# State updates of sample sequences on 32-row groups of the TensorE array, in place of zero-padded 128-row tiles

## The chip, the cores and the metric

The kernel runs on one core of a Trainium2 chip. The metric is the device time of one execution in microseconds (us); lower is better. Times of a kernel are given as the median of several runs.

## What is computed

One decoder layer: gated linear attention (GLA) beside causal pooling, merged by gates, then a feed-forward block. It runs for one prompt of 256 tokens and for eight sample sequences of 8 new tokens each, which share all weights. The change lies in the GLA state of the samples. Cut to what matters (`D_MODEL` is 2048, so there are 4 heads with `DK_HEAD` 256 and `DV_HEAD` 512, and `DEC_BATCH` is 8):

```python
kd = k * jnp.exp(b_last - b)              # decayed keys
decay = jnp.exp(b_last[:, :, :, 0, :])
...
def step(s, inp):
    qe_n, kd_n, v_n, dec_n = inp
    o = jnp.einsum('bhcd,bhde->bhce', qe_n, s)
    s = dec_n[..., None] * s + jnp.einsum('bhcd,bhce->bhde', kd_n, v_n)
    return s, o
```

For each sample sequence and each head the new state is a 256x512 matrix: the old one times a decay per row, plus the product of the sequence's decayed keys (tokens x 256) with its values (tokens x 512).

## The kernel before, in words

**The bulk.** Activations lie transposed, features on partitions, with all 320 tokens (256 of the prompt, 64 of the samples) along the free axis. Every projection is a stream of matmuls on 128x128 weight tiles and 320 columns. To reach float32 accuracy each weight chunk is split into a high and a low part in the `float32r` format (`split`, L142: ACT writes `whi` at L147, DVE writes `wlo` at L148), and three matmuls stand in place of one (`mm3`, L160: L161 `whi`·high, L162 `whi`·low, L163 `wlo`·high). This stream fills TensorE (PE) nearly from end to end. It is called the main stream below.

**The side work.** After the first head's projections, the loop over heads 1 to 3 (L904) runs the main stream of one head while the attention and pooling steps of the head before it are mixed in: `queue` holds small functions, and `pump` (L887) calls ten of them after each projection. `gla_steps` (L541) makes the list. The Tile scheduler then decides the order on each engine from its own time model, so that the side work's matmuls stand one by one or in small groups between those of the main stream. Their results go to PSUM tiles `pm` of 128x512, one bank each, of which there are four in turn (`misc`, L98).

**The state update.** The eight sequences are handled in two halves `gg` of four sequences `j`. Each sequence owns 32 rows: `kdP` holds its decayed keys (8 high parts, the same again, the 8 low parts, the same again), and `vp` (L665) its values in the matching arrangement, so that one product over 32 rows gives the product at full accuracy. `s_kpn(gg)` (L683) turns the keys of four sequences round by two transposes (`tr`, L123, whose matmul is recorded at L125) and then builds `kpn`, of shape 128 x 4 x 256: POOL clears it (L686), and for each `j` the 32 rows of that sequence are copied into column block `j`, by DVE (L694) for odd `j` and by ACT (L696) for even `j`. All other rows of block `j` stay zero. `s_state(gg, d, j0)` (L762) then takes, for two sequences, the matmul of L767: weights are 128 rows by 128 columns of `kpn`, the moving operand all 128 rows of `vp` by 512 columns; the zeros take out the three other sequences. DVE adds the result to the decayed state (L769), and when the second pair of a tile is done POOL issues the store (L771). Per head there are 2 halves x 2 column blocks `d` x 4 sequences, 64 such matmuls in the program. The page names `kpn` as `w`, after its pool tag.

**Tiles of the array.** Four other places hand a `tile_position` to a matmul: L221 and L281 (conditioning), L645 (attention of the prompt) and L746 (read-out of the sample states). All of these use weights of 32 columns at column offset 0, 32, 64 or 96 and all 128 rows, four side by side. No place uses a row offset.

Of the kernel before, what the change touches and what calls it, by code (L numbers as in the profile page):

```python
# [11 lines left out]
F32 = mybir.dt.float32  # L12
F32R = mybir.dt.float32r
# [7 lines left out]
P = 128  # L21
# [7 lines left out]
H, DK, DV = 4, 256, 512  # L29
# [50 lines left out]
def body(tc, A):  # L80
# [13 lines left out]
    def nm(s):  # L94
        uid[0] += 1
        return "%s_%d" % (s, uid[0])

    def misc():  # L98
        return pmisc.tile([P, 512], F32, tag="m", name=nm("pm"))

    V, S, G, PE = nc.vector, nc.scalar, nc.gpsimd, nc.tensor
# [21 lines left out]
    def tr(out, in_):  # L123
        k = in_.shape[0]
        PE.transpose(out, in_, ident[:k, :k])  # L125
# [273 lines left out]
    with tc.tile_pool(name="head", bufs=1) as xp:  # L399
# [9 lines left out]
        pt = misc()  # L409
# [22 lines left out]
        pt = misc()  # L432
# [105 lines left out]
    def w4(shape, dt=F32):  # L538
        return lp.tile(shape, dt, tag="w4", bufs=4, name=nm("w4"))

    def gla_steps(g):  # L541
        h = g.h
        st = []
        E = {}
# [137 lines left out]

        def s_kpn(gg):  # L683
            def f():
                kpn = E["kpn"] = w4([P, 4, DK], F32R)
                G.memset(kpn.bitcast(F32), 0.0)  # L686
                pt = misc()
                for d in range(2):
                    tr(pt[:, d * P:(d + 1) * P],
                       kdP[:, d, 4 * gg:4 * gg + 4, :].rearrange("p b r -> p (b r)").bitcast(F32))  # L690
                for j in range(4):
                    sl = slice(32 * j, 32 * j + 32)
                    if j % 2:
                        V.tensor_copy(kpn[sl, j, :], pt[sl, 0:DK])  # L694
                    else:
                        S.copy(kpn[sl, j, :], pt[sl, 0:DK])  # L696
            return f

        def s_o(e2):
# [62 lines left out]
        def s_state(gg, d, j0):  # L762
            def f():
                t = E["S0", gg, d]
                for j in (j0, j0 + 1):
                    pt = misc()
                    PE.matmul(pt, lhsT=E["kpn"][:, j, d * P:(d + 1) * P], rhs=E["vp"][:, gg], start=True, stop=True)  # L767
                    c = 4 * gg + j
                    V.scalar_tensor_tensor(t[:, j], t[:, j], E["dec"][:, d, c:c + 1], pt, op0=ALU.mult, op1=ALU.add)  # L769
                if j0 == 2:  # L770
                    nc.gpsimd.dma_start(A["o_gs"][0, 4 * gg:4 * gg + 4, h, d * P:(d + 1) * P, :]  # L771
                                        .rearrange("b p e -> p b e"), t)
            return f
# [119 lines left out]
    st, E = gla_steps(g0)  # L893
# [10 lines left out]
    for h in range(1, H):  # L904
        pump(RATE)
        g = new_group(h)
        for ui, (kind, i, col) in enumerate(units(h)):
# [5 lines left out]
            if kind == "u":  # L913
                pump(len(queue))
                st, E = gla_steps(g)
# [96 lines left out]
    for pi, (f0, f1) in enumerate(parts):  # L1012
# [31 lines left out]
        for ui in range(8):  # L1044
            ps = proj(wdn, 256 * ui, f0, f1, ah, al)
            for i in range(2):
                k = 2 * ui + i
                residual(ps, i, k, 5)
                if pi == 1:
# [3 lines left out]
                    pt = misc()  # L1053
# [9 lines left out]
    pt = misc()  # L1063
# [9 lines left out]
    for a in range(3):  # L1073
        n = P if a < 2 else TS
        for c in range(2):
            sl = yn[a][:n, c * 1024:(c + 1) * 1024]
# [28 lines left out]
```

## Time and profile before

| what | value |
|---|---|
| device time, median of 3 runs | 1989.61 us (1988.78 to 1991.63) |
| span of the profiled execution | 1989.4 us |
| PE busy | 1938.0 us, 97% of the span |
| DVE busy | 1002.8 us, 50% |
| ACT busy | 829.4 us, 42% |
| POOL busy | 179.3 us, 9% |
| matmuls | 13808 |

The profile is of one execution, whose own time is its span, from the first instruction to the last. PE is the matmul, PEld the loading of its weights, which can go on beside the matmul before it. A matmul's row shows its duration from start to modelled end, which includes the time through the array, so that neighbours overlap: a main stream matmul is listed at 0.31 us though one ends every 0.15 us. The chain of waits is the view that shows how far one instruction moves the end: each of its pieces runs from the end of the piece before it to its own end.

### The profile page before, as it was taken

The page shows a single profiled execution, that of the slowest core. Times are in us where ns is not written, and L with a number is a line of the kernel's source. Part 1 is how long each engine was busy: PE and PEld are TensorE (multiplying, and loading weights), DVE is VectorE, ACT ScalarE, POOL GpSimd, SP SyncE. Part 2 cuts the span into 40 slices and gives each one's busy share as a digit, 9 for nine tenths or more (in the row PEclk, how much of TensorE's full clock was granted, in tenths as well). Part 3 has the DMA queues.
Part 4 walks back from the last instruction along what each step waited for, and adds up shares of the span by engine and source line. Part 5 has one row for each costly group of instructions (what it writes and reads, how often), then busy time and mean ns, then how long its engine had stood idle before and what let it go on. Part 6 is the DMA issues. An engine that isn't in the chain of part 4 may idle for free.

```text
span 1989.4 us, 34665 instructions
## 1 busy us (share of the span) xinstructions
PE 1938.0 (97%) x13808; PEld 1819.7 (91%) x13808; DVE 1002.8 (50%) x1918; ACT 829.4 (42%) x1483; POOL 179.3 (9%) x292
## 2 busy tenths in 40 slices
PE   5999999999999999999999999999999999999997
PEld 3778998889999889989979999999999999999997
DVE  2655645656356635665574444444444444444554
ACT  3323633544336433653344333433333434344443
POOL 1002101212121112111130000000000000000000
PEclk9999999999999999999999999999999999999998
DMA  9997458758975888479836555444444444444443
GB/s 316 344 333 239 141 170 281 231 182 288 302 221 171 274 283 257 148 248 329 265 100 197 185 185 178 156 147 145 150 148 154 149 151 151 152 150 140 149 141 101
DMA packets 309276, 400.59 MB, mean 201 GB/s; under 512 B 12418, under 2 KB 273058, under 8 KB 308778
## 3 DMA queue, kind: packets, MB, share of 16 engines
q1 hardware_dynamic: 279754, 291.17, 46.8%
q0 software_dynamic: 29360, 107.21, 15.6%
q8 instruction: 108, 1.77, 0.4%
q14 instruction: 54, 0.43, 0.1%
HBM read 373.90 MB, written 24.67 MB: 200 GB/s over the span
## 4 chain that ended last, share of the span: by engine, by line
PE 90%; DMA 6%; DVE 2%; ACT 1%; issue 0%; SPq 0%; POOL 0%; ACTq 0%; DVEq 0%
PE ps L161 26%; PE ps L163 26%; PE ps L162 26%; PE pm L281 3%; DMA araw<-w_ada 2%; DMA raw<-w_in 2%; PE pm L125 2%; PE pm L221 1%; DMA raw<-w_o 1%; PE pm L767 1%; PE pm L746 1%; PE pm L715 1%; DMA vr<-b_ada 1%; DVE wlo L148 1%; ACT whi L147 0%
## 5 line engine op out<-in xcount | busy, mean ns | idle before, releaser
L148 DVE TENSOR_TENSOR wlo<-raw,whi 128x512 fp32r<-128x512 f32 x952 | 654.9, 692 | 804.8 <-ACT whi L147 801.3
L147 ACT CAST whi<-raw 128x512 fp32r<-128x512 f32 x952 | 586.2, 622 | 923.3 <-PE ps L162 811.2
L161 PE MATMUL ps<-hh,whi 128*128 128x320 f32 x1408 | 443.1, 315 | 4.2 <-ACT whi L147 3.2
L162 PE MATMUL ps<-hl,whi 128*128 128x320 f32 x1408 | 439.2, 312 | 0.0
L163 PE MATMUL ps<-hh,wlo 128*128 128x320 f32 x1408 | 436.6, 312 | 1.3 <-DVE wlo L148 1.3
L161 PE MATMUL ps<-h2h,whi 128*128 128x320 f32 x1408 | 435.7, 310 | 0.0
L162 PE MATMUL ps<-h2l,whi 128*128 128x320 f32 x1408 | 435.5, 309 | 0.0
L163 PE MATMUL ps<-h2h,wlo 128*128 128x320 f32 x1408 | 435.4, 309 | 0.0
L161 PEld LDWEIGHTS ps<-hh,whi 128*128 128x128 f32 x1408 | 264.9, 188 | 28.2 <-issue 16.2
L163 PEld LDWEIGHTS ps<-hh,wlo 128*128 128x128 f32 x1408 | 264.2, 188 | 13.7 <-issue 7.3
L162 PEld LDWEIGHTS ps<-hl,whi 128*128 128x128 f32 x1408 | 265.1, 188 | 5.4 <-issue 4.6
L161 PEld LDWEIGHTS ps<-h2h,whi 128*128 128x128 f32 x1408 | 264.3, 188 | 3.4 <-ACT ah L317 3.4
L162 PEld LDWEIGHTS ps<-h2l,whi 128*128 128x128 f32 x1408 | 264.3, 188 | 0.0
L163 PEld LDWEIGHTS ps<-h2h,wlo 128*128 128x128 f32 x1408 | 264.3, 188 | 0.0
L161 PE MATMUL ps<-ah,whi 128*128 128x320 f32 x704 | 217.7, 309 | 0.0
L162 PE MATMUL ps<-al,whi 128*128 128x320 f32 x704 | 216.5, 308 | 0.0
L163 PE MATMUL ps<-ah,wlo 128*128 128x320 f32 x704 | 216.5, 308 | 0.0
L162 PEld LDWEIGHTS ps<-al,whi 128*128 128x128 f32 x704 | 132.0, 187 | 0.0
L161 PEld LDWEIGHTS ps<-ah,whi 128*128 128x128 f32 x704 | 131.9, 187 | 0.0
L163 PEld LDWEIGHTS ps<-ah,wlo 128*128 128x128 f32 x704 | 131.9, 187 | 0.0
L255 POOL DMA_DIRECT2D araw<-w_ada x64 | 54.9, 862 | 448.5 <-PE pm L281 419.2
L161 PE MATMUL ps<-mh,whi 128*128 128x320 f32 x256 | 79.5, 310 | 0.7 <-ACT whi L147 0.7
(280 smaller groups left out, 1609.4 us busy)
## 6 DMA issues: line engine op xcount, KB each, us to landing
raw<-w_gu SPq DMA_DIRECT2D x176, 512.0 KB, 3.5
raw<-w_in SPq DMA_DIRECT2D x173, 512.0 KB, 4.5
araw<-w_ada POOLq DMA_DIRECT2D x64, 1024.0 KB, 8.5
raw<-w_down SPq DMA_DIRECT2D x80, 512.0 KB, 3.5
raw<-w_ada SPq DMA_DIRECT2D x64, 512.0 KB, 6.6
S<-state_gla POOLq DMA_DIRECT2D x16, 1024.0 KB, 9.6
o_gs<-S POOLq DMA_DIRECT2D x16, 1024.0 KB, 5.9
raw<-w_o SPq DMA_DIRECT2D x32, 512.0 KB, 5.1
```

The source lines that it names most:

```text
L125: PE.transpose(out, in_, ident[:k, :k])
L147: S.copy(hi, raw)
L148: V.tensor_sub(lo, raw, hi.bitcast(F32))
L161: PE.matmul(ps, lhsT=whi, rhs=xhi, start=start, stop=False)
L162: PE.matmul(ps, lhsT=whi, rhs=xlo, start=False, stop=False)
L163: last_mm[:] = [PE.matmul(ps, lhsT=wlo, rhs=xhi, start=False, stop=stop).ins]
L221: PE.matmul(ps[32 * j:32 * j + 32, 0:w], lhsT=scT[:, k0 + i, :], rhs=raw[:, i, :], start=r == 0, stop=r == 3, tile_position=(0, 32 * j))
L255: nc.gpsimd.dma_start(t[:, r:r + step], wada[:, k0 + r:k0 + r + step, col:col + nb * P])
L281: PE.matmul(ps[32 * j:32 * j + 32, 0:w], lhsT=scT[:, k0 + r + j, :], rhs=ada_raw[n][:, r + j, :], start=k0 == 0 and first, stop=k0 + nk == ...
L715: PE.matmul(pt, lhsT=E["kdn"][:, s, d * P:(d + 1) * P], rhs=E["vn"][:, s], start=s == 0, stop=s == 1)
L746: PE.matmul(pt[32 * j:32 * j + 32, :], lhsT=qeP[:, d, 4 * gg + j, :], rhs=E["S0", gg, d][:, j], start=False, stop=d == 0, tile_position=(0 ...
L767: PE.matmul(pt, lhsT=E["kpn"][:, j, d * P:(d + 1) * P], rhs=E["vp"][:, gg], start=True, stop=True)
```

## The change

`kpn` becomes one unpadded tile of 128 x 256: the transposed keys of four sequences are copied into it as they are, by one ACT copy, and neither the clearing nor the three other copies are made. Each matmul of `s_state` takes as weights only the 32 rows of its sequence, and as moving operand the same 32 rows of `vp`, and is placed at row offset 32·j of the array by `tile_position`. The two matmuls of a pair are written before the two DVE updates instead of in turn with them; their two `pm` tiles are taken together.

```diff
         def s_kpn(gg):
             def f():
-                kpn = E["kpn"] = w4([P, 4, DK], F32R)
-                G.memset(kpn.bitcast(F32), 0.0)
+                kpn = E["kpn"] = w4([P, DK], F32R)
                 pt = misc()
                 for d in range(2):
                     tr(pt[:, d * P:(d + 1) * P],
                        kdP[:, d, 4 * gg:4 * gg + 4, :].rearrange("p b r -> p (b r)").bitcast(F32))
-                for j in range(4):
-                    sl = slice(32 * j, 32 * j + 32)
-                    if j % 2:
-                        V.tensor_copy(kpn[sl, j, :], pt[sl, 0:DK])
-                    else:
-                        S.copy(kpn[sl, j, :], pt[sl, 0:DK])
+                S.copy(kpn, pt[:, 0:DK])
             return f
...
         def s_state(gg, d, j0):
             def f():
                 t = E["S0", gg, d]
-                for j in (j0, j0 + 1):
-                    pt = misc()
-                    PE.matmul(pt, lhsT=E["kpn"][:, j, d * P:(d + 1) * P], rhs=E["vp"][:, gg], start=True, stop=True)
+                pts = [misc(), misc()]
+                for j, pt in zip((j0, j0 + 1), pts):
+                    r = slice(32 * j, 32 * j + 32)
+                    PE.matmul(pt, lhsT=E["kpn"][r, d * P:(d + 1) * P], rhs=E["vp"][r, gg], start=True, stop=True,
+                              tile_position=(32 * j, 0))
+                for j, pt in zip((j0, j0 + 1), pts):
                     c = 4 * gg + j
                     V.scalar_tensor_tensor(t[:, j], t[:, j], E["dec"][:, d, c:c + 1], pt, op0=ALU.mult, op1=ALU.add)
```

The changed lines shift those below: the matmul of L767 is L762 after. How the scheduler places the matmuls is seen in the order on PE. At the start of a group of eight (the first head, `gg` 0; `pm` is the result, `vp` the values, `w` is `kpn`, `ps` the main stream's result) PE has before:

```order
L125 MATMUL pm_3220<-cst,adasb_3221 128x128 x2
L767 MATMUL pm_3229<-vp_2953,w_506_2981 128x512
L767 MATMUL pm_3232<-vp_2953,w_506_2981 128x512
L767 MATMUL pm_3235<-vp_2953,w_506_2981 128x512
L162 MATMUL ps_3321<-hl_104,whi_3340 128x320
```

and after:

```order
L125 MATMUL pm_3216<-cst,adasb_3217 128x128 x2
L762 MATMUL pm_3225<-vp_2953,w_506_2981 128x512
L762 MATMUL pm_3226<-vp_2953,w_506_2981 128x512
L762 MATMUL pm_3231<-vp_2953,w_506_2981 128x512
L162 MATMUL ps_3317<-hl_104,whi_3336 128x320
```

Nothing has moved here: the first pair and the first of the second pair stand side by side in both. All eight groups of eight begin so. The five others of the same group stand, some 20 rows on, before:

```order
L161 MATMUL ps_3321<-hh_91,whi_3374 128x320
L767 MATMUL pm_3238<-vp_2953,w_506_2981 128x512
L162 MATMUL ps_3321<-hl_107,whi_3374 128x320
L163 MATMUL ps_3321<-hh_91,wlo_3375 128x320
L161 MATMUL ps_3321<-hh_92,whi_3374 128x320
L162 MATMUL ps_3321<-hl_108,whi_3374 128x320
L767 MATMUL pm_3242<-vp_2953,w_506_2981 128x512
L163 MATMUL ps_3321<-hh_92,wlo_3375 128x320
L161 MATMUL ps_3321<-hh_92,whi_3374 128x320
L162 MATMUL ps_3321<-hl_108,whi_3374 128x320
L767 MATMUL pm_3245<-vp_2953,w_506_2981 128x512
L163 MATMUL ps_3321<-hh_92,wlo_3375 128x320
```

and after:

```order
L161 MATMUL ps_3317<-hh_91,whi_3370 128x320
L762 MATMUL pm_3232<-vp_2953,w_506_2981 128x512
L162 MATMUL ps_3317<-hl_107,whi_3370 128x320
L163 MATMUL ps_3317<-hh_91,wlo_3371 128x320
L161 MATMUL ps_3317<-hh_92,whi_3370 128x320
L162 MATMUL ps_3317<-hl_108,whi_3370 128x320
L762 MATMUL pm_3238<-vp_2953,w_506_2981 128x512
L163 MATMUL ps_3317<-hh_92,wlo_3371 128x320
L161 MATMUL ps_3317<-hh_92,whi_3370 128x320
L162 MATMUL ps_3317<-hl_108,whi_3370 128x320
L762 MATMUL pm_3239<-vp_2953,w_506_2981 128x512
L163 MATMUL ps_3317<-hh_92,wlo_3371 128x320
```

Here too the order stays: each of these five stands alone between main stream matmuls, the two of a pair (`pm_3238` and `pm_3239` after) with three matmuls of the main stream between them. Over the whole program the 64 matmuls stand in 48 places, 8 of three and 40 of one, in both kernels.

Elsewhere on PE one thing moves twice (heads 1 and 2): a run of eight column-tiled matmuls of L645. Before, it is whole:

```order
L162 MATMUL ps_4684<-hl_104,whi_4703 128x320
L645 MATMUL pm_4100<-w_706_4104,EQK_3942 32x128 x3
L645 MATMUL pm_4100<-EQK_3942 32x128
L645 MATMUL pm_4100<-w_706_4104,EQK_3942 32x128 x3
L645 MATMUL pm_4100<-EQK_3942 32x128
L163 MATMUL ps_4684<-hh_88,wlo_4704 128x320
```

After, one matmul of the main stream stands in its middle:

```order
L162 MATMUL ps_4668<-hl_102,whi_4671 128x320
L645 MATMUL pm_4088<-w_706_4092,EQK_3934 32x128 x3
L645 MATMUL pm_4088<-EQK_3934 32x128
L163 MATMUL ps_4668<-hh_86,wlo_4672 128x320
L645 MATMUL pm_4088<-w_706_4092,EQK_3934 32x128 x3
L645 MATMUL pm_4088<-EQK_3934 32x128
L161 MATMUL ps_4668<-hh_86,whi_4671 128x320
```

So the runs of column-tiled matmuls number 92 before and 94 after.

## The prediction

> **What bounds the kernel now.** I read the page first, then the table of stages, then the chain of waits in the stage of the change. The page's first lines, and the chain's shares by line:
>
> ```profile
> span 1989.4 us, 34665 instructions
> PE 1938.0 (97%) x13808; PEld 1819.7 (91%) x13808; DVE 1002.8 (50%) x1918; ACT 829.4 (42%) x1483; POOL 179.3 (9%) x292
> PE 90%; DMA 6%; DVE 2%; ACT 1%; issue 0%; SPq 0%; POOL 0%; ACTq 0%; DVEq 0%
> ```
>
> PE is busy for 97% of the span and holds 90% of the chain. An average may hide stages, so the table by stages comes next, cut at 270 and 900 us, since the 64 matmuls of L767 start between 302.5 and 871.3 us:
>
> ```profile
> core 0: us, PE busy (x) PEld busy (x) DVE busy (x) ACT busy (x) POOL busy (x), PEclk, DMA share, GB/s
> 270.00:900.00 630.00, 624.08 (x4637) 564.29 (x4637) 345.55 (x685) 283.50 (x524) 109.10 (x157) 1.00 0.74 239
> ...
> L767 PEld LDWEIGHTS pm<-vp,w x64: 187/188/192, 302.5 to 871.2; 128*128 128x128 f32 x64
> L767 PE MATMUL pm<-vp,w x64: 388/393/482, 302.5 to 871.3; 128*128 128x512 f32 x64
> ```
>
> In this stage PE stands idle for 630.0 − 624.1 = 5.9 us, while DVE is busy for 55%, ACT for 45% and POOL for 17% of it. So PE alone sets the end here: what PE gains or loses between 270 and 900 us, the kernel gains or loses, and what the other engines gain is worth nothing as long as PE does not come to wait for them. What an instruction of PE costs is its piece in the chain:
>
> ```profile
> 302.53 0.22 PE pm L125 x2
> 302.75 0.71 PE pm L767 x3
> 303.46 0.15 PE ps L162
> ...
> 305.96 0.15 PE ps L161
> 306.11 0.23 PE pm L767
> 306.34 0.15 PE ps L162
> ```
>
> A state matmul costs 0.23 us, alone or in a row of three (0.71 us, of which the first holds 0.01 more); one of the main stream costs 0.15 us. There is no loss at the border between the two: both are whole-array matmuls, and the next weights (0.19 us to load, the row above) are loaded beside the running matmul. All 64 together take about 64 x 0.23 = 14.7 us of PE's time.
>
> **The change part by part.** *The copies and the clearing.* These rows of the groups by shape are the work around `kpn`:
>
> ```profile
> L686 POOL MEMSET w<- 128x1024 f32 x8 | 7.7, 966 | 0.0
> L694 DVE CAST w<-pm 32x256 fp32r<-32x256 f32 x16 | 6.8, 423 | 5.8 <-ACT w L696 5.4
> L696 ACT CAST w<-pm 32x256 fp32r<-32x256 f32 x16 | 5.8, 361 | 2.8 <-DVE w L694 1.3 <-PE pm L125 1.3
> L290 ACT COPY adasb<-pm 128x256 f32<-128x256 f32 x32 | 11.9, 372 | 30.7 <-PE pm L281 28.1 <-PE pm L125 2.4
> L769 DVE SCALAR_TENSOR_TENSOR S<-S,dec,pm 128x512 f32<-128x512 f32 x64 | 46.0, 742 | 0.7
> ```
>
> POOL loses 7.7 us, DVE 6.8 us, and ACT goes from 5.8 us to eight copies of the size of L290's, 8 x 0.37 = 3.0 us. I count all of it as nothing: the cover is PE's own backlog, with 5.9 us of idle time in 630. These edits only take away, so if the cover were gone they could give at most a part of those 5.9 us. `kpn` is ready after one copy instead of four that followed one another. The 64 DVE updates stay as they are, and DVE has 45% of the stage free for results that come in bunches. The new order of writing adds no instruction and no DMA, and moves none of the 64 matmuls past another queue's work.
>
> *Matmuls side by side.* Of a place with three, all lie on different rows of the array (0, 32, 64) and write different banks. The trace has no row tiles, so the gain is bounded: by nothing, if they run one after the other, and by the nearest row, the column tiles of L746, if they overlap:
>
> ```profile
> 285.53 0.86 PE pm L742 x2
> 286.39 1.85 PE pm L746 x16
> 288.24 0.34 PE ps L161
> 288.58 0.15 PE ps L162
> ```
>
> L742 is a whole-array matmul of 512 columns in plain float32, 0.86/2 = 0.43 us. Sixteen column tiles of the same 512 columns take 1.85 us, which is four times 0.43 and 0.13 left over: four tiles that lie on different parts of the array cost one. By that row a place of three costs 0.23 us plus little, say 0.25 in place of 0.71, and eight such places give 8 x 0.46 = 3.7 us. I take this end, since it is the same kind of packing. The 40 that stand alone have nothing to overlap with: the order of the new program puts three or more main stream matmuls, which use all rows, between them. So 24 of the 32 pairs are pairs in the code only.
>
> In the Trainium skill, "TensorE: Matmul & The Clock Gate", section "Part 3: Packing small matmuls — row/col tiling", four 32-row tiles of 512 columns ran 3.07 times as fast as one after the other. Estimated by that, three would gain a little less than I count; no run here shows row tiles yet.
>
> *Going in and out.* The same rows show what a tiled run costs at its ends. The 0.13 us left over in L746's piece is the way in, and the main stream matmul behind it takes 0.34 in place of 0.15 us: the way out costs 0.19. A second place shows the same with other sizes:
>
> ```profile
> 311.20 0.15 PE ps L162
> 311.35 0.57 PE pm L645 x16
> 311.92 0.64 PE pm L650 x4
> 312.56 0.44 PE pm L125 x4
> ```
>
> L125's whole-array matmuls of 128 columns cost 0.11 us each. Sixteen tiles of L645 with 128 columns should cost 4 x 0.11 = 0.44; they cost 0.57, so 0.13 for the way in. The four passes of L650 should cost 0.44 and cost 0.64, so 0.20 for the way out. The two ways differ in the weights that are loaded first in the new shape, and these rows show how long a load is:
>
> ```profile
> L746 PEld LDWEIGHTS pm<-S,qeP x128: 106/110/110, 286.3 to 857.8; 128*32 128x32 f32 x128
> ...
> 7.09 1.87 PE L125 MATMUL pm<-cst,junk 9*128 9x9 f32 x16 [7.09 <-POOL cst masks.py:199]
> ```
>
> On the way in weights of 32 columns are loaded (0.11 us), on the way out weights of 128 columns (0.19 us): a difference of 0.08 against 0.07 in the two costs. I read this as a wait until the array is empty, followed by a load that nothing hides. The new row tiles load 32 rows by 128 columns. That fewer rows make a load no shorter is seen in the transposes at the start: with only 9 rows they still take 1.87/16 = 0.12 us each, no less than the 0.11 of 128 rows. So the way in should cost a row tile what the way out costs, 0.20.
>
> For row tiles the cost is unknown, and bounded by nothing (rows may need no such wait) and by 0.20 + 0.19 = 0.39 us a place; the column tiles as they are give 0.13 + 0.19 = 0.32. I take 0.39, because the row it is nearest to is that of a tile shape that changes, and the loads are wide on both sides. Every one of the 48 places stands between whole-array matmuls in the new order, so each pays both ways: 48 x 0.39 = 18.7 us. A tiled run split in two more places (L645 in two heads, 92 runs to 94) adds 2 x 0.33 = 0.7 us.
>
> The Trainium skill, "TensorEngine Tiling (Array Packing)", section "Key Properties", says that changing the tiling mode, not just the tile, drains TensorE, and its section "Available Configurations" lists 32-row tiles as modes of their own. The column tiles of this trace agree, with 0.13 and 0.19 us; the page gives no price, and it speaks against a change that goes in and out 48 times.
>
> *The sum.* 18.7 + 0.7 − 3.7 = +15.7 us on the profiled 1989.4, so 2005.1. The median of the runs is 1989.6, 0.2 above the profiled span: **2005.3 us**. With 0.32 a place it is +12.4, 2002.0.
>
> **The rivals.**
>
> *Rows need no switch.* Then only the gain and the split runs are left, −3.7 + 0.7 = −3.0 us: 1986.6, a change of 0.15%. For it speaks that not every narrow matmul pays. These, of the small projection at L482, have weights of 64 columns and stand among the main stream's:
>
> ```profile
> 179.33 0.29 PE ps L161 x2
> 179.62 0.15 PE pm L161
> 179.77 0.15 PE pm L162
> 179.91 0.15 PE ps L162
> ```
>
> They cost 0.15 us like their neighbours, going in and out. Against it: they name no place in the array, while all the matmuls that do name one pay, and the new ones name one.
>
> *Only one way pays.* A small tile could wait for the whole array to come free, while the way back finds three quarters of it free already, or the reverse. Then 48 x 0.20 = 9.6, and 9.6 + 0.7 − 3.7 = +6.6 us: 1996.2.
>
> *The switch is paid and nothing overlaps*, because the three moving operands come one after the other. Then the 3.7 us are missing: +19.4, 2009.0.
>
> *The pairs do overlap, all of them.* This would need the hardware to bring 24 split pairs together past the matmuls between; then 32 x 0.22 = 7.0 us faster, 1982.6. Every piece of the chain in this stage follows the program's order, so I give it almost nothing.
>
> The side on which the change ends is decided by the price of a place: it breaks even at 3.0 / 48 = 0.06 us.
>
> **How the numbers follow.** A measurement of this kernel can tell about 0.2%, 4.0 us, from no change. My forecast, 2002 to 2006 by the price of a place, gets 0.70; one way only 0.08; paid without overlap 0.05; no switch 0.16; all pairs 0.01. The first three are slower by more than 4.0 us, 0.83 together. No switch is −3.0 us, within the bound but near it: 0.12 of it same, 0.04 faster, and with the last rival faster has 0.05. The range reaches from one way only, 1996, to paid without overlap, 2009, and leaves out the last two, 0.17.
>
> **What would show it right or wrong.** In the chain after: a lone L762 piece should be about 0.43 us (0.23 + 0.20) and the main stream piece behind it 0.34; a place of three about 0.45 in place of 0.71. If lone pieces stay at 0.23 with 0.15 behind them, rows need no switch. If a place of three takes 0.9 or more, nothing overlaps. PE's idle time in the stage should stay near 6 us; if it grows by more than a few us behind DVE's or ACT's work, the cover that I named is not there. The prediction is wrong if the time is below 1996.

## The result, and the profile after

| | median us | runs | ratio to before, 95% interval |
|---|---|---|---|
| before | 1990.03 | 5 (1988.78 to 1991.63) | |
| after | 2011.88 | 5 (2010.36 to 2021.16) | 1.0112 [1.0099, 1.0124] |

The change costs 21.9 us. The side was forecast; the size was not: 2005.3 was named, with 2009 as the upper end, and the measured time lies 6.6 us above the one and 2.9 us above the other. A device time is 1.7 to 2.3 us above the span of the same execution in all runs (1991.63 belongs to the span of 1989.4, 2021.16 to 2019.4), so differences of spans and differences of times can be set side by side. The profiled execution of after is the longest of its five; a profile of the same kernel taken later has a span of 2010.2. I therefore read single pieces from the first and sums from several.

The first lines of the page of after, and the shares of the chain by engine:

```profile
span 2019.4 us, 34610 instructions
PE 1959.9 (97%) x13808; PEld 1821.3 (90%) x13808; DVE 998.5 (49%) x1902; ACT 825.5 (41%) x1475; POOL 170.8 (8%) x284
PE 88%; DMA 7%; DVE 2%; ACT 2%; issue 1%; SPq 0%; POOL 0%; ACTq 0%; DVEq 0%; POOLq 0%
```

PE is still the engine that ends last, but the shares of DMA and ACT in the chain have each gone up by one in a hundred (6% and 1% before). The chain at the first group of eight shows the price of a place (start, length, what):

```profile
302.64 0.22 PE pm L125 x2
302.86 0.44 PE pm L762 x2
303.30 0.35 PE ps L162
303.65 0.14 PE ps L163
...
305.99 0.15 PE ps L161
306.14 0.43 PE pm L762
306.57 0.34 PE ps L162
306.91 0.15 PE ps L163
```

A lone matmul moves the end by 0.43 where it was 0.23, the main stream matmul behind it by 0.34 where it was 0.15: 0.20 in and 0.19 out, as forecast. A place of three (the chain counts two of them, the third ends with them) takes 0.44 in place of 0.71. By the instruction rows, all 40 lone places cost 0.39 us more than before and the eight places of three, with the matmul behind them, 0.07 less: 15.1 us together, where the prediction's two terms, 18.7 less 3.7, give 15.0. The rows of L762 (ns, least, median, most) show the load that is paid on the way in:

```profile
L762 PEld LDWEIGHTS pm<-vp,w x64: 181/181/182, 302.8 to 893.6; 32*128 32x128 f32 x64
```

A load of 32 rows takes 181 ns where one of 128 rows took 188: a quarter of the rows saves next to nothing, as the transposes at the start had suggested. That each way of the switch is such a load which nothing hides fits these sizes (0.18 of 0.20 us); no run takes the load and the wait for an empty array apart.

What was not forecast is seen in the table of the stage, cut at a place where PE stands still (us, then the busy time of PE, PEld, DVE, ACT and POOL, then PE's granted clock and the DMA share):

```profile
270.00:490.00 220.00, 215.41 (x1507) 181.28 (x1506) 118.77 (x234) 91.87 (x168) 37.59 (x56) 0.99 0.68 227
490.00:505.00 15.00, 12.07 (x64) 11.81 (x64) 6.68 (x13) 3.85 (x7) 0.00 (x0) 0.77 0.72 234
505.00:920.00 415.00, 413.75 (x3054) 368.86 (x3054) 213.13 (x417) 183.59 (x340) 63.25 (x93) 1.00 0.71 232
```

PE is idle for 4.6 + 2.9 + 1.3 = 8.8 us where before had 5.9, and 2.9 us of it lie in one place near 495 us, with 15 us at a mean clock of 0.77 around it. Before, the same place had next to no idle time, at full clock:

```profile
480.00:495.00 15.00, 14.83 (x119) 13.37 (x119) 9.84 (x19) 6.03 (x13) 1.59 (x3) 1.00 0.83 267
```

The chain there after, and PE's own row (in brackets its idle time and what ended it):

```profile
487.01 9.45 DMA raw<-w_in
...
497.08 0.61 ACT whi L147
497.70 0.61 ACT mg L382
498.31 0.04 issue
498.35 0.64 PE psy L161
498.99 0.27 PE psy L162
```

```profile
498.35 0.64 PE L161 MATMUL psy<-dh,whi 128*128 128x320 f32 x1 [2.93 <-ACT mg L382]
```

A weight load of the main stream takes 9.45 us to land (the median of its kind is 4.5), ACT casts it, ACT then evacuates a gate projection (L382), and only then may the pooling matmul (`psy`) go on, since it writes to the PSUM tile that L382 has emptied. After that a main stream matmul takes 0.27 us instead of 0.15. ACT's timeline in after:

```profile
485.03 1.14 ACT L147 CAST whi<-raw 128x512 fp32r<-128x512 f32 x2 [6.33 <-PE pm L281]
486.08 0.36 ACT L290 COPY adasb<-pm 128x256 f32<-128x256 f32 x1
486.73 1.14 ACT L147 CAST whi<-raw 128x512 fp32r<-128x512 f32 x2 [0.28 <-DVE wlo L148]
488.06 0.62 ACT L147 CAST whi<-raw 128x512 fp32r<-128x512 f32 x1 [0.19 <-PE ps L162]
490.04 0.62 ACT L147 CAST whi<-raw 128x512 fp32r<-128x512 f32 x1 [1.36 <-PE ps L162]
496.56 1.14 ACT L147 CAST whi<-raw 128x512 fp32r<-128x512 f32 x2 [5.90 <-DMA raw<-w_in]
497.60 0.70 ACT L382 ACTIVATE mg<-ps 128x640 f32<-128x640 f32 x1
```

And the same place in before:

```profile
479.04 1.14 ACT L147 CAST whi<-raw 128x512 fp32r<-128x512 f32 x2 [7.66 <-DMA raw<-w_in]
480.09 0.36 ACT L290 COPY adasb<-pm 128x256 f32<-128x256 f32 x1
480.38 1.14 ACT L147 CAST whi<-raw 128x512 fp32r<-128x512 f32 x2
482.30 0.62 ACT L147 CAST whi<-raw 128x512 fp32r<-128x512 f32 x1 [0.79 <-PE ps L162]
484.06 0.62 ACT L147 CAST whi<-raw 128x512 fp32r<-128x512 f32 x1 [1.14 <-PE ps L162]
484.59 0.70 ACT L382 ACTIVATE mg<-ps 128x640 f32<-128x640 f32 x1
489.91 1.14 ACT L147 CAST whi<-raw 128x512 fp32r<-128x512 f32 x2 [4.62 <-DMA raw<-w_in]
```

Both kernels have a pause of ACT of 6 to 8 us here (ahead of 479.04 and of 485.03), at a column-tiled run of L281, the conditioning, whose result L290 copies out. What differs is where the pause stands in the stream of chunks. The order on ACT, in which two casts make one chunk and `mg` is the first gate half, before and after:

```order
L382 ACTIVATE mg_122<-ps_4850 128x640
L147 CAST whi_5085<-raw_5083 128x512
L147 CAST whi_5101<-raw_5083 128x512
L147 CAST whi_5119<-raw_5117 128x512
L147 CAST whi_5135<-raw_5117 128x512
L290 COPY adasb_4842<-pm_4824 128x256
```

```order
L382 ACTIVATE mg_122<-ps_4834 128x640
L147 CAST whi_5069<-raw_5067 128x512
L147 CAST whi_5085<-raw_5067 128x512
L290 COPY adasb_4826<-pm_4808 128x256
```

One chunk more stood ahead of L290 before. On PE, the four runs of L281 at the gate projections of head 1 start 12 or 13 matmuls of L161 to L163 earlier in the program of after (the first behind 2030 of them, where it was 2042), and twelve is what one `whi` tile feeds. So it isn't the case, as was said ahead of the prediction, that elsewhere on PE only the two runs of L645 move: by the order of the two programs some 460 of the 12873 matmul instructions stand elsewhere. A cast frees the buffer into which SP loads a later chunk, so what ACT has not cast ahead of the pause, SP cannot ask for ahead of it. The first chunk of the next head is asked for at 472.13 us in before, ahead of the pause:

```profile
472.13 0.37 SPq L139 DMA_DIRECT2D raw<-w_in  x1
```

In after that is at 487.01, behind the pause (the DMA piece of the chain above), and the chunk lands at 496.46. In before the late chunk is the next one, behind L382, and nobody waits for it. In after it is the pair of casts just ahead of L382, and L382 waits with it.

### The profile page after: what moved, and what is told of

Read it like the earlier page. It is cut to its first block, busy times and chain, and to the rows that moved or that the text cites. A ratio compares the mean times of both kernels' runs of the same rounds, so it can differ in the third digit from the quotient of the medians.

```text
span 2019.4 us, 34610 instructions
## 1 busy us (share of the span) xinstructions
PE 1959.9 (97%) x13808; PEld 1821.3 (90%) x13808; DVE 998.5 (49%) x1902; ACT 825.5 (41%) x1475; POOL 170.8 (8%) x284
## 4 chain that ended last, share of the span: by engine, by line
PE 88%; DMA 7%; DVE 2%; ACT 2%; issue 1%; SPq 0%; POOL 0%; ACTq 0%; DVEq 0%; POOLq 0%
PE ps L161 26%; PE ps L163 26%; PE ps L162 25%; PE pm L281 3%; DMA raw<-w_in 3%; DMA raw<-w_o 2%; PE pm L125 2%; PE pm L221 1%; PE pm L762 1%; PE pm L740 1%; DMA vr<-b_ada 1%; PE pm L709 1%; DMA o_gs<-S 1%; DVE wlo L148 1%; DMA araw<-w_ada 1%
## 5 line engine op out<-in xcount | busy, mean ns | idle before, releaser
L161 PE MATMUL ps<-hh,whi 128*128 128x320 f32 x1408 | 444.6, 316 | 5.2 <-ACT whi L147 4.1
L163 PE MATMUL ps<-hh,wlo 128*128 128x320 f32 x1408 | 441.5, 316 | 1.7 <-DVE wlo L148 1.7
L161 PE MATMUL ps<-h2h,whi 128*128 128x320 f32 x1408 | 435.4, 309 | 0.0
L163 PE MATMUL ps<-h2h,wlo 128*128 128x320 f32 x1408 | 434.7, 309 | 0.0
L161 PEld LDWEIGHTS ps<-hh,whi 128*128 128x128 f32 x1408 | 265.4, 189 | 28.8 <-issue 18.2
L163 PEld LDWEIGHTS ps<-hh,wlo 128*128 128x128 f32 x1408 | 264.6, 188 | 21.3 <-issue 14.3
L161 PEld LDWEIGHTS ps<-h2h,whi 128*128 128x128 f32 x1408 | 264.3, 188 | 4.2 <-ACT ah L317 3.4
L163 PEld LDWEIGHTS ps<-h2h,wlo 128*128 128x128 f32 x1408 | 264.4, 188 | 0.0
L161 PE MATMUL ps<-ah,whi 128*128 128x320 f32 x704 | 217.7, 309 | 0.0
L163 PE MATMUL ps<-ah,wlo 128*128 128x320 f32 x704 | 216.5, 308 | 0.0
L161 PEld LDWEIGHTS ps<-ah,whi 128*128 128x128 f32 x704 | 131.9, 187 | 0.0
L163 PEld LDWEIGHTS ps<-ah,wlo 128*128 128x128 f32 x704 | 131.9, 187 | 0.0
L161 PE MATMUL ps<-mh,whi 128*128 128x320 f32 x256 | 79.6, 311 | 5.8 <-ACT whi L147 5.8
```

The costliest lines, as they stand in the source:

```text
L161: PE.matmul(ps, lhsT=whi, rhs=xhi, start=start, stop=False)
L163: last_mm[:] = [PE.matmul(ps, lhsT=wlo, rhs=xhi, start=False, stop=stop).ins]
```

## The experiments

Theory: the switch costs 0.39 us a place, three matmuls overlap, and the rest of the loss comes from the new order of everything else, which puts PE behind late loads and then at half clock. Rivals: the rest belongs to the row tiles themselves (a switch that costs more than the chain shows), or to scatter between chips; further, that nothing overlaps. Three sets of runs, each on one chip with the kernel before beside it (1991.74, 1991.61 and 1990.35 us).

**The scatter.** Before and after once more, without an edit.

> The kernel before, unchanged, to see its span and granted clock run by run. Theory S (the switch into and out of row tiles is the whole loss, and the rest of the measured 21.9 us is chance: late loads and half-clock stretches that come and go): spans of the runs of before scatter by several us too, with the granted clock between 0.993 and 0.997. Rival R (the change itself brings idle time of PE and half-clock stretches): all runs of before stay at a granted clock of 0.996 and within 2 us of each other, and the profile has at most two half-clock stretches of 3.4 us between 270 and 1100 us.

> The changed kernel, unchanged, for a second profile. Theory S: the idle stretches of PE at 495 us (2.9 us) and 942 us (5.8 us) are gone or elsewhere, lone state matmuls again take 0.43 us and the matmul behind them 0.34, and the span of this execution without idle time and half-clock stretches is 15 to 16 us above that of before. Rival R: the same two idle stretches are there again, and with them more than 10 us of half clock.

Measured: 1992.82 us for before, ratio 0.9998 [0.9988, 1.0007]; 2012.18 for after, 1.0097 [1.0082, 1.0112]. The loss stands, at +20.4. The span of the profiled before was 1993.4 here, so one execution can lie 4 us from another. Of what was expected of after, neither side came true as a whole: the stop of PE near 495 us is there again in the second profile of after, with 2.9 us, and the one near 942 us is not. So the first belongs to the kernel, and nothing shows that the second does.

**The new order alone, with the whole array.**

```diff
-                    r = slice(32 * j, 32 * j + 32)
-                    PE.matmul(pt, lhsT=E["kpn"][r, d * P:(d + 1) * P], rhs=E["vp"][r, gg], start=True, stop=True,
-                              tile_position=(32 * j, 0))
+                    PE.matmul(pt, lhsT=E["kpn"][:, d * P:(d + 1) * P], rhs=E["vp"][:, gg], start=True, stop=True)
```

> The changed kernel with whole-array state matmuls: all 128 rows of the unpadded keys and values, no row offset. It leaves out the selection of one sequence (each state gets the sum over the four of its half); the copies, the tiles and the order of instructions are those of the changed kernel. Theory S: 16 us faster than the changed kernel, that is within 2 us of before, lone state matmuls 0.23 us and 0.15 behind them. Rival R (the other edits or the new order bring the loss that the switch does not explain): 4 to 7 us slower than before.

Measured: 1995.77 us, ratio 1.0025 [1.0012, 1.0037]. All instructions stand in the order of after, and the chain shows the price of before:

```profile
305.76 0.23 PE pm L761
305.99 0.15 PE ps L162
```

The row tiles are gone and +4.0 us stay. This part of the loss is the order's (by the interval of the ratio between 2.4 and 7.4 us), and its profile has the stop in front of the pooling matmul too (2.3 us, behind L382).

**The row tiles alone, in the old order.** Before, with the clearing and the four copies kept; the weights are the sequence's own rows of its padded block.

```diff
-                    PE.matmul(pt, lhsT=E["kpn"][:, j, d * P:(d + 1) * P], rhs=E["vp"][:, gg], start=True, stop=True)
+                    r = slice(32 * j, 32 * j + 32)
+                    PE.matmul(pt, lhsT=E["kpn"][r, j, d * P:(d + 1) * P], rhs=E["vp"][r, gg], start=True, stop=True,
+                              tile_position=(32 * j, 0))
```

> The kernel before with one edit: each state matmul takes only the 32 rows of its sequence, at row offset 32 j, from the padded tile. Copies, clearing and the order on every engine are those of before. Theory: the loss has two parts that add up, the switch (48 x 0.39 - 3.7 = 15.0 us) and the new order of the other work (about 5 us, seen when the whole array is kept). Then this kernel is 15 us slower than before, 2005 to 2009 us beside a before of 1990 to 1993, and the PE idle stretch in front of the pooling matmuls near 495 us is not there. Rival (the whole loss comes with the row tiles, the idle stretch too): 19 to 21 us slower.

Measured: 2006.16 us, ratio 1.0065 [1.005, 1.008], +14.6 by the medians and +10 to +16 by the interval. The sum that was forecast, less the 0.7 for the split runs, is 15.0. The table of its stage has no stop where after has one:

```profile
485.00:505.00 20.00, 19.84 (x169) 17.46 (x160) 10.84 (x20) 7.58 (x14) 3.52 (x4) 1.00 0.82 258
```

So the row tiles bring about 15 us, and what lifts the loss to 20.4 to 23.5 in the three sets that have after in them is the rest of the edit, which the prediction counted at nothing. The two parts taken alone, 14.6 and 4.0, add up to 18.6; the 2 to 5 us that are left no single run accounts for.

**Do the three overlap?** After, with every row tile on the first 32 rows.

```diff
-                    r = slice(32 * j, 32 * j + 32)
+                    r = slice(0, 32)
...
-                              tile_position=(32 * j, 0))
+                              tile_position=(0, 0))
```

> The changed kernel with every state matmul on rows 0 to 31 (all four states of a half get the first sequence's product). The 48 ways in and out stay, but no two matmuls lie on different rows. If different rows overlap as read from the profile after: places of three take 0.43 + 2 x 0.23 = 0.89 us instead of 0.43, 8 x 0.46 = 3.7 us slower than the changed kernel. If the overlap were an artefact of modelled ends: no difference.

Measured: 2014.96 us, ratio 1.0112 [1.0096, 1.0129], 2.8 us above after on the same chip, where 3.7 were expected; the four runs of after all lie below these four. The chain at the place that took 0.44:

```profile
302.53 0.89 PE pm L762 x3
303.42 0.34 PE ps L162
```

On the same rows the three take 0.89 = 0.20 + 3 x 0.23; on different rows 0.44. Overlap is worth 0.45 a place, 3.6 us over eight, and the switch is paid either way.

**Only where three stand together.** Before, with row tiles for `d == 0 and j < 3` alone, which are the eight places of three.

```diff
+                    if d == 0 and j < 3:
+                        r = slice(32 * j, 32 * j + 32)
+                        PE.matmul(pt, lhsT=E["kpn"][r, j, d * P:(d + 1) * P], rhs=E["vp"][r, gg], start=True, stop=True,
+                                  tile_position=(32 * j, 0))
+                    else:
...
```

> The kernel before with row tiles only in the eight places where three state matmuls stand side by side; the 40 lone ones keep the whole array. Order on every engine as before. By the prices of the profile after (place 0.43 in place of 0.71, next matmul 0.34 in place of 0.15): 8 x (0.19 - 0.28) = -0.7 us, no difference that can be measured. If a switch cost more than the pieces of the chain show (clock, later stalls): slower by several us.

Measured: 1990.99 us, ratio 0.9993 [0.9983, 1.0002]. Switch and overlap cancel, as worked out; the gain, if there is one, is too small for the measurement.

**Pairs made to stand together.** The two results of a pair share one two-bank PSUM tile, and the second matmul is put right behind the first: 32 places of two. The second kernel has the same order with whole-array matmuls.

```diff
+                pp = pstate.tile([P, 2, 512], F32, tag="st", name=nm("pst"))
+                pts = [pp[:, 0], pp[:, 1]]
...
+                    with tc.high_priority() if j > j0 else nullcontext(), tc.issue_after(first) if j > j0 else nullcontext():
```

> The changed kernel with the two results of a pair in one PSUM tile of two banks (misc tiles go from four to two), so that all 32 pairs stand side by side: 32 places of two. 13 of them stand right behind a run of column tiles and 3 between two such runs. If a step from column tiles to row tiles costs one switch, not two: places of two among whole-array matmuls lose 0.39 - 0.22 = 0.17 us each (16 of them), those behind a column run gain 0.02, those between two gain 0.22; +1.8 us beside the next kernel, which differs in the row offset alone. If each place costs both ways wherever it stands: +5.4 us.

> The same as the kernel of 32 places of two, with whole-array state matmuls (it leaves out the selection of one sequence). Same order on every engine. Switch theory: 1.8 us faster than that kernel; if every place costs both ways: 5.4 us faster.

Measured: 2004.1 us, ratio 1.0053 [1.0038, 1.0068], with row tiles, and 2001.23, 1.0045 [1.0028, 1.0062], without. Both lose to before for another reason: PE is idle for some 10 us more, which I put down to the smaller PSUM pools without a run that shows it. The difference of the two is the question here. By the medians it is 2.9 us (1.6 by the ratios), nearer to 1.8 than to 5.4, but the runs of the two overlap, and their profiles differ by as much in work at half clock alone (the table below), so the time doesn't settle it. The instruction rows of the 32 places do: summed up, they differ by 1.3 us. At a place that follows the column tiles of L741, the chain with row tiles:

```profile
335.99 1.29 PE pm L741 x12
337.27 0.42 PE pst L765
337.70 0.35 PE ps L164
```

and with whole-array matmuls:

```profile
332.15 1.29 PE pm L741 x12
333.44 0.67 PE pst L764 x2
334.11 0.15 PE ps L164
```

Behind column tiles the whole-array pair pays the way out itself: 0.67 = 0.20 + 2 x 0.23. The row-tiled pair pays 0.42, one switch, no dearer than from the whole array. Over the pair and the matmul behind it that is 0.77 against 0.82: here a pair of row tiles is already the cheaper, while behind the main stream it is the dearer (0.78 against 0.62 by the instruction rows). Of the 32 places 16 stand behind a column-tiled run, 3 of them between two.

**The stop itself.** After, with the casts of the next head's first chunk put behind L382 on ACT. No operation is added; in the order of the whole program 10 places on ACT, 14 on DVE and 24 on PE differ, since four runs of L281 shift by one matmul as well.

```diff
+        with tc.issue_after(hold[0]) if len(hold) == 2 else nullcontext():
+            S.copy(hi, raw)
...
-            S.activation(gb, src, AF.Sigmoid)
+            hold[:] = [S.activation(gb, src, AF.Sigmoid).ins]
```

> The changed kernel, with one thing moved: at the end of head 1 the ACT evacuation of the last gate projection stands ahead of the two weight casts of the next head's first chunk, not behind them. Nothing is left out. Theory (the rest of the loss is one evacuation queued on ACT behind casts that wait for a late weight load): the cast will still wait some 5 us for its load, but the pooling matmul near 492 us will not; of the 2.9 us of idle most goes, and with it the half-clock stretch that follows (6.8 us at half speed, up to 3.4 us): 3 to 6 us less than the changed kernel, 2006 to 2009. Rival (the rest is spread over the row tiles, or over loads that are late anyway): the idle time only moves to the next matmul that needs the late chunk, and the time stays within 2 us of the changed kernel.

> The changed kernel as it is, on the same chip as the two kernels with the moved evacuation, so that they can be set against it: both theories 2010 to 2013, 19 to 22 us over the kernel before, with 2 to 3 us of idle time in front of a pooling matmul near 492 us and a half-clock stretch behind it.

Measured: 2007.66 us, ratio 1.0083 [1.0069, 1.0098], and after on the same chip 2013.85, 1.0118 [1.0103, 1.0134]: 6.2 us less, just above the 3 to 6 that were expected, and no run of the one reaches a run of the other (2005.42 to 2009.58, 2012.49 to 2018.44). The rival falls. ACT's timeline with the move:

```profile
487.74 0.62 ACT L150 CAST whi<-raw 128x512 fp32r<-128x512 f32 x1 [1.36 <-PE ps L165]
491.41 0.70 ACT L385 ACTIVATE mg<-ps 128x640 f32<-128x640 f32 x1 [3.05 <-PE ps L166]
494.43 1.14 ACT L150 CAST whi<-raw 128x512 fp32r<-128x512 f32 x2 [2.32 <-DMA raw<-w_in]
```

and the table of its stage at that place:

```profile
487.00:502.00 15.00, 14.91 (x123) 13.74 (x122) 7.95 (x18) 5.12 (x9) 1.75 (x2) 1.00 0.90 297
```

The cast still waits for the load, the evacuation (L385 here) does not, PE stands still for 0.1 us instead of 2.9 (3.4 in the after of the same chip), and the clock stays at 1.00. Not all of the gain in the profiles is the move's: a stretch of 3.4 us at half clock near 378 us, ahead of the moved place, is absent as well, which is worth 1.7 us.

**The same move with the whole array.**

> The same move in the kernel with whole-array state matmuls in the new order (it leaves out the selection of one sequence, as that kernel does; same work in time). Theory: the new order's +4 to 5 us shrink to 0 to 2 us over the kernel before, 1991.5 to 1993.5 at a before of 1991.5. Rival: it stays at +4 to 5 us.

Measured: 1996.16 us, ratio 1.0024 [1.0014, 1.0034]. The theory missed: +5.8 stay. PE's timeline shows why:

```profile
492.44 0.30 PE L166 MATMUL psy<-dh,wlo 128*128 128x320 f32 x1
494.79 1.84 PE L284 MATMUL pm<-araw,scT 128*32 128x256 f32 x22 [2.05 <-DMA araw<-w_ada]
```

The pooling matmuls no longer wait, but the column-tiled run behind them does, for a 1 MB load that has not landed. With row tiles PE comes there at 494.89 and finds it landed; without them it is 2.1 us earlier. The stop does not belong to L382 but to the loads that are late: L382 was the one thing that waited in after. That an idle time closed at one place opens at the next when PE is early is how this reads; no run set the loads themselves earlier.

## Why the prediction was wrong in size and right in side

One sum holds the runs together. For each profiled execution I take the idle time of PE between 200 and 1700 us (1500 less its busy time in the table, which for before and after reads as below) and, in the same window, the time that PE worked while the granted clock was 0.5. About half of that time is lost, since a main stream matmul takes 0.27 us in it instead of 0.15.

```profile
200.00:1700.00 1500.00, 1487.27 (x10552) 1408.66 (x10551) 764.01 (x1410) 642.25 (x1142) 152.89 (x237) 1.00 0.62 199
```

```profile
200.00:1700.00 1500.00, 1479.92 (x10351) 1380.46 (x10351) 746.82 (x1377) 626.85 (x1115) 144.52 (x229) 0.99 0.60 196
```

| profiled execution, against before (span 1989.4, idle 12.7, work at half clock 6.8) | span | idle | half of work at half clock | rest |
|---|---|---|---|---|
| before again | +4.0 | +2.2 | +1.0 | +0.8 |
| only where three stand together | −2.2 | −0.4 | 0.0 | −1.8 |
| new order, whole array | +9.7 | +4.2 | +4.5 | +1.1 |
| the same, L382 moved | +8.2 | +1.8 | +5.9 | +0.5 |
| old order, row tiles | +16.8 | −1.3 | +1.3 | +16.8 |
| after, L382 moved | +16.7 | +0.2 | −0.3 | +16.8 |
| after, second profile | +20.8 | +2.7 | +2.2 | +16.0 |
| after, third profile | +23.9 | +2.3 | +4.2 | +17.5 |
| after, first profile | +30.0 | +7.4 | +6.0 | +16.7 |
| after, all on the first rows | +27.5 | +5.1 | +1.4 | +21.0 |
| pairs side by side, row tiles | +12.9 | +9.8 | +3.6 | −0.5 |
| pairs side by side, whole array | +9.3 | +10.4 | +0.7 | −1.8 |

The rest is put down to what the matmuls themselves take. It is good to about 1 us, as the second profile of before shows. With row tiles it is 16.0 to 17.5, where 15.7 was forecast (15.0 in the old order); with whole-array matmuls in the order of before or after it is 0.5 to 1.1; with row tiles only where three stand together −1.8, where −0.7 was worked out; with nothing overlapping it is 21.0, where 19.4 was. Between the two kernels with pairs it differs by 1.3.

- *The price of a place*, 0.39 us, taken from column tiles: right, 0.20 and 0.19 in the chain. That was not certain from the traces of before, which bounded it by nothing and 0.39; the choice of the upper end was an argument, and it held. The rivals without a switch, or with one way only, fall with it.
- *Overlap of three*, −3.7 us: right. The experiment on the same rows gives 3.6 by the chain, 2.8 by the medians. Nothing brings split pairs together: each lone matmul pays by itself.
- *The split runs of L645*, +0.7: they are column-tiled runs like the others; no run tried them alone, and the rest above is too coarse to show 0.7.
- *"I count all of it as nothing: the cover is PE's own backlog"*: this step failed. That ACT, DVE and POOL save work was rightly worth nothing. But the scheduler decides the order of everything from its time model, and what was removed moves that order. It is the clearing on POOL that does it. Built with the clearing and the four copies kept and the pairs written first, the program has the order of before on every engine; with the clearing kept and one copy in place of four, it has the order of before too, but for the copies; without the clearing and with the four copies, it has the order of after. These are readings of built programs; no run timed them one by one. I followed the 64 matmuls ("moves none of the 64 matmuls past another queue's work") and L645, not the other matmuls and not ACT's queue. The step went on to say that edits which only take away could at best give a part of 5.9 us. They took 4.0 us with the whole array, and with row tiles 6 to 9 us by the medians, the loss of after less the 14.6 of the old order. The profiles show where: idle time and half clock together are +4.9, +6.4 and +13.3 in the three of after, and 0.0 in the old order.
- *PE's idle time in the stage* was the sign named in advance: it should stay near 6 us. It went to 8.8, and the stop was the longest new one.
- *The base*: the profiled execution of before took 1991.63, not its span, so the step from span to median was 2 us off in its wording; the sum of 15.7 stands on the median either way.

What stays open is how large the order's part is on another day: it depends on when the loads land, and idle time of after varies from 15.0 to 20.1 us between three profiles of the same program, with an extra 5.8 us at 942 us in the first, behind a weight load that took 17.8 us to land.

## What to carry to other kernels

A tiled place in a stream of whole-array matmuls costs a price of its own, here 0.39 us for tiles of 32 rows by 128 columns, so count places and not matmuls: three side by side just pay for it, one alone costs 0.62 in place of 0.23, and a place next to another tiled run has the switch half paid. When an edit takes work away from idle engines under a scheduler (here one clearing per half, on an engine that was idle for 83% of the stage), compare the order of all instructions on all engines, above all of those that ask for loads or free buffers, and not only of those that were edited. And what stands behind a wait in an engine's queue is part of that wait, as L382 behind the two casts was: look at the instruction after each one that waits for a load.

## What the runs showed of the hardware

- Row tiles on different rows start 3 to 4 ns apart by the instruction rows, and three of 512 columns cost 0.24 us after the switch (0.44 less 0.20), against 0.71 one after the other, some 2.9 times as fast. The Trainium skill, "TensorE: Matmul & The Clock Gate", section "Part 3: Packing small matmuls — row/col tiling", gives 3.07 times for four row tiles of 512 columns, that is 0.77 of their number; three here come to some 0.97 of theirs.
- From column tiles to row tiles is one switch (0.42 for the pair, as from the whole array), and so is the reverse: 0.23 us for the first column tile of L646 behind a row-tiled pair, and the same behind a whole-array one.
- Short idle times can cost as much again in clock. After 2.9 us of idle the clock stood at half for 6.8 us, after 2.05 us for 3.4; but after 2.25 us in the kernel with L382 moved it did not fall at all:

```profile
372.00:382.00 10.00, 7.39 (x50) 6.87 (x49) 7.63 (x17) 4.19 (x7) 5.92 (x13) 1.00 0.74 215
```

and after 2.05 us in the kernel with the whole array and L382 moved it did:

```profile
491.00:501.00 10.00, 7.95 (x63) 6.15 (x63) 5.74 (x13) 2.13 (x4) 1.75 (x2) 0.83 0.68 213
```

- The Trainium skill, "TensorE: Matmul & The Clock Gate", section "Why this matters for your kernels", advises against idle gaps of over some 3 us between bursts of matmuls. Here gaps of 2 us were enough, though not each time: in the kernel with all tiles on the first rows even 3.68 us, near 1046 us, were not followed by it (granted clock 1.00 from 1040 to 1060 us).
